# A token's norm factor enters a decoder layer's opening by a diagonal matrix on TensorE

## The chip, the cores and the metric

The kernel runs on one core of one Trainium2 chip. The metric is device time in microseconds (us) of one execution. The engines are TensorE (PE; its weight loads are listed apart, as PEld), VectorE (DVE), ScalarE (ACT), GpSimd (POOL) and SyncE (SP), which here only issues transfers. Each engine works through its own queue in order. A product on TensorE writes to PSUM, which is eight banks of 128 partitions by 512 fp32 columns.

## The reference

One layer of a decoder on 512 tokens of width 2048, all in fp32: a norm, one input projection whose columns feed gated linear attention (GLA) and differential softmax attention, an output projection, a norm and the residual, then a gated feed-forward part of 5632 with a short convolution, again between norms. The change concerns the first norm and the first 512 columns that are projected:

```
h = rmsnorm(x, attn_pre_norm)    # x * rsqrt(mean(x*x) + 1e-6) * g, by token
proj = h @ w_in                  # 512 x 2048 by 2048 x 6160
```

A token's h is x times one factor of that token, times the gain row g, which is the same for all tokens.

## The kernel before

Tokens are held in four tiles of 128 (t = 0 to 3), one token to a partition. For the projections h is needed transposed, its 2048 columns on partitions in 16 slots, and in two parts: `ah` (the value rounded to fp32r, which TensorE multiplies in one instruction) and `al` (the rest). Every weight piece of 128x1024 is split in the same way: ACT copies the high part (L148), DVE subtracts it for the low part (L149). A product is then three matmuls, ah by high, ah by low, al by high (L202 to L204, 512 columns each).

`first_half` is the opening. It computes the first 512 projected columns while x, the gain row and the first weights arrive, and it does this for the first 1024 columns of h of every tile, then for the second 1024, always in pieces of 512 columns (`H4`). Its order is written out by hand, and PE, ACT, DVE, POOL and SP run it as written:

- The gain row is brought to all partitions. Its first 1024 columns come by a small transfer to one partition and a product with a matrix that has ones in one row (`spread`, L260: an fp32 product into a bank, once for each 512 columns), and DVE copies the bank to `gb` (L261). The other 1024 come by a transfer. Transpositions of the identity (`warm`, L267) keep TensorE busy before and after.
- For each tile ACT squares x with a running sum (`square_by` for tiles 0 and 1, L275; `square` for 2 and 3, L285), DVE and POOL make of the sums the token's factor `rs` (L277, L278, L280; POOL's power is L280).
- DVE multiplies x by the factor and the gain row at once (`scale`, L292).
- PE transposes four 128x128 blocks into a bank (`turn`, through `transpose_into_act`, L169), and ACT and DVE split the bank into `ah` and `al` (L161, L162).
- PE multiplies (`prods`, `mm_n`).

So every tile goes squares, factor, scaling, transposition, split, products. For tile 0 this chain ends later than its data, and for tile 1 it begins once ACT is through with the first weights. From tile 2 on the products of the tiles before lie beside it. `transpose_into_act` is used a second time, much later, for the second norm.

Behind the opening a scheduler places the rest (the other projections, the gate and constants that are prepared meanwhile) by a model of time; from about 107 us its order on PE is the same in both programs. The later lines that the prediction names: L605 (GLA scores by block, an fp32 product of 128x128 by 128x128, once for each of four blocks and four heads), L403 (a DVE multiplication of a 128x256 tile by a number), L493 (the transposition of small constants, among them rows of the convolution's bias).

Of the kernel before, what the change touches and what calls it, by code (L numbers as in the profile page):

```python
# [9 lines left out]
F32 = mybir.dt.float32  # L10
F32R = mybir.dt.float32r
U8 = mybir.dt.uint8
AF = mybir.ActivationFunctionType
ALU = mybir.AluOpType
# [3 lines left out]
P = 128  # L18
D = 2048
S = 512  # L20
NT = S // P
# [14 lines left out]
def hybrid_layer(ctx: ExitStack, tc: tile.TileContext, x, attn_pre_norm, w_in, w_alpha_up, b_alpha,  # L36
# [3 lines left out]
    nc = tc.nc  # L40
    x2, out2 = x[0], out[0]
# [5 lines left out]
    def dma(o, i):  # L47
        return nc.sync.dma_start(out=o, in_=i)
# [3 lines left out]
    act = nc.scalar.activation  # L52
    tt = nc.vector.tensor_tensor
    ts = nc.vector.tensor_scalar
    stt = nc.vector.scalar_tensor_tensor
    mm = nc.tensor.matmul

    const = ctx.enter_context(tc.tile_pool(name="const", bufs=1))
    small = ctx.enter_context(tc.tile_pool(name="small", bufs=8, side="right"))
# [5 lines left out]
    ident = few.tile([P, P], F32, name="ident")  # L65
# [11 lines left out]
    def bank(pool=None):  # L77
        return (pool or psa).tile([P, 512], F32, name="bank", tag="bank")
# [31 lines left out]
    def load(src, a, by=None):  # L110
        raw = wpool.tile([P, GR], F32, name="raw", tag="raw", bufs=4)
        (by or nc.sync).dma_start(out=raw.rearrange("p (a b) -> p a b", a=a), in_=src)
        return raw
# [25 lines left out]
    def granule(src, a, raw=None, spare=None, hl=None):  # L139
        if raw is None:  # L140
            raw = load(src, a)
        if hl is not None:
            hi, lo = hl[:, 0, :], hl[:, 1, :]
        elif spare:
            hi, lo = spare_halves(spare)
        else:
            hi, lo = halves()
        act(hi, raw, AF.Copy)  # L148
        tt(lo, raw, hi.bitcast(F32), ALU.subtract)  # L149
        r = "p (a b) -> p a b"  # L150
        return hi.rearrange(r, a=a), lo.rearrange(r, a=a)

    def rsqrt_mean(ss, n, width=1):
        t = small.tile([P, width], F32, name="ms", tag="ms")
        nc.gpsimd.tensor_scalar(t, ss, 1.0 / n, EPS, ALU.mult, ALU.add)
        r = small.tile([P, width], F32, name="rs", tag="rs")
        nc.gpsimd.tensor_tensor(r, t, nhalf[:, :width], ALU.pow)
        return r

    def split(hi, lo, src):  # L160
        act(hi, src, AF.Copy)  # L161
        tt(lo, src, hi.bitcast(F32), ALU.subtract)  # L162

    def transpose_into_act(src, t, slot0, n):
        for g in range(0, n, 4):
            m = min(4, n - g)
            b = bank()
            for j in range(m):
                nc.tensor.transpose(b[:, j * P:(j + 1) * P], src[:, (g + j) * P:(g + j + 1) * P], ident)  # L169
            bv = b[:, :m * P].rearrange("p (k c) -> p k c", k=m)  # L170
            split(ah[:, t, slot0 + g:slot0 + g + m, :], al[:, t, slot0 + g:slot0 + g + m, :], bv)

    def bcast_row(tile_ap, row):
        dma(tile_ap, row.partition_broadcast(P))
# [23 lines left out]
    def mm_n(banks, t, g, w, slots=tuple(range(KT)), ks=(0, 1)):  # L198
        for k in ks:
            i = 2 * g + k  # L200
            st, sp, s = i == 0, i == KT - 1, slots[i]
            mm(banks[t], ah[:, t, s, :], w[0][:, k, :], start=st, stop=False)  # L202
            mm(banks[t], ah[:, t, s, :], w[1][:, k, :], start=False, stop=False)  # L203
            mm(banks[t], al[:, t, s, :], w[0][:, k, :], start=False, stop=sp)  # L204
# [15 lines left out]
    bp = boot.enter_context(tc.tile_pool(name="boot", bufs=6))  # L220

    def big8(name, dt=F32):
        return bp.tile([P, 2048], dt, name=name, tag="big8", bufs=6)


    def first_half(c):
        gb = big8("gb")
        jb = bp.tile([P, 1024], F32, name="jb", tag="jb", bufs=1)
        xts = [big8("xt") for _ in range(NT)]
        w3 = big8("w3", F32R).rearrange("p (h x) -> p h x", h=2)  # L230
        H2 = [slice(1024 * i, 1024 * (i + 1)) for i in range(2)]
        H4 = [slice(512 * i, 512 * (i + 1)) for i in range(4)]
        rs, raws, w = {}, {}, {}
        banks = [bank(psm) for _ in range(NT)]
        col = C_GV + 512 * c

        def load_x(t):
            for i in range(2):
                dma(xts[t][:, H2[i]], x2[t * P:(t + 1) * P, H2[i]])

        def load_w(*gs):
            for g in gs:
                raws[g] = load(w_in3[:, 2 * g:2 * g + 2, col:col + 512], 2)

        def weights(g):
            w[g] = granule(None, 2, raws[g], hl=w3 if g == 3 else None)

        def gain_row():
            row = gb[:, H2[1]]
            one = xts[3][:, :P]  # L250
            nc.vector.memset(row[:, :512], 0.0)
            nc.gpsimd.memset(row[:, 512:], 0.0)
            nc.vector.memset(one, 0.0)
            nc.vector.memset(one[:1], 1.0)
            nc.scalar.dma_start(out=row[:1], in_=attn_pre_norm[0:1, H2[0]])

            def spread():
                for i in range(2):
                    b = bank()
                    mm(b, one, row[:, H4[i]], start=True, stop=True)  # L260
                    nc.vector.tensor_copy(gb[:, H4[i]], b)  # L261
            return spread

        def warm(n):
            b = bank()
            for i in range(n):
                nc.tensor.transpose(b[:, (i % 4) * P:(i % 4 + 1) * P], ident, ident)  # L267

        def square_by(t, n):
            q = small.tile([P, 2], F32, name="ss2", tag="ss2", bufs=4)  # L270
            if n > 2:
                q = xts[3][:, P:P + n]
            m = 2048 // n
            for i in range(n):
                act(jb[:, :m], xts[t][:, m * i:m * (i + 1)], AF.Square, accum_out=q[:, i:i + 1])  # L275
            ss = small.tile([P, 1], F32, name="ss", tag="ss")
            nc.vector.reduce_sum(ss, q, axis=AX.X)  # L277
            ts(ss, ss, 1.0 / D, EPS, ALU.mult, ALU.add)  # L278
            rs[t] = small.tile([P, 1], F32, name="rs", tag="rs")
            nc.gpsimd.tensor_tensor(rs[t], ss, nhalf[:, :1], ALU.pow)  # L280

        def square(t):
            ss = small.tile([P, 2], F32, name="ss2", tag="ss2", bufs=4)
            for i in range(2):
                act(jb, xts[t][:, H2[i]], AF.Square, accum_out=ss[:, i:i + 1])  # L285
            sm = small.tile([P, 1], F32, name="ss", tag="ss")
            nc.gpsimd.tensor_tensor(sm, ss[:, 0:1], ss[:, 1:2], ALU.add)
            rs[t] = rsqrt_mean(sm, D)

        def scale(t, *ps):  # L290
            for i in ps:
                stt(xts[t][:, H4[i]], xts[t][:, H4[i]], rs[t], gb[:, H4[i]], ALU.mult, ALU.mult)  # L292

        def turn(t, *ps):
            for i in ps:
                transpose_into_act(xts[t][:, H4[i]], t, 4 * i, 4)

        def prods(t, *gs):
            for g in gs:
                mm_n(banks, t, g, w[g])  # L300

        spread = gain_row()
        for i in range(4):
            dma(xts[0][:, H4[i]], x2[:P, H4[i]])
        load_w(0, 1, 2, 3)
        load_x(1)
        load_x(2)
        warm(11)
        spread()
        warm(9)  # L310
        square_by(0, 4)
        load_x(3)
        bcast_row(gb[:, H2[1]], attn_pre_norm[0, H2[1]])
        scale(0, 0, 1)
        weights(0)
        turn(0, 0)
        weights(1)
        turn(0, 1)
        weights(2)
        weights(3)  # L320
        square_by(1, 2)
        prods(0, 0, 1, 2, 3)
        scale(1, 0, 1)
        turn(1, 0, 1)
        square(2)
        square(3)
        scale(2, 0, 1)
        prods(1, 0, 1, 2)
        mm_n(banks, 1, 3, w[3], ks=(0,))
        turn(2, 0, 1)  # L330
        mm_n(banks, 1, 3, w[3], ks=(1,))
        scale(3, 0, 1)
        prods(2, 0, 1)
        scale(0, 2, 3)
        turn(3, 0, 1)
        prods(2, 2)
        scale(1, 2, 3)
        turn(0, 2, 3)
        prods(2, 3)
        scale(2, 2, 3)  # L340
        turn(1, 2, 3)
        prods(3, 0, 1)
        scale(3, 2, 3)
        turn(2, 2, 3)
        prods(3, 2)
        turn(3, 2, 3)
        prods(3, 3)
        return banks
# [44 lines left out]
    for li, hs in enumerate(LEVELS):  # L393
        nb = 64 // hs
        m = ms[:, 64 * li:64 * (li + 1)]
# [25 lines left out]
    rows = tmp("rows")[:NF, :].rearrange("p (a d) -> p a d", a=4)  # L421
# [735 lines left out]
    m = [wp.tile([P, D], F32, name=f"m{t}") for t in range(NT)]  # L1157
# [808 lines left out]
```

## Time and profile before

| | |
|---|---|
| median of 3 runs | 2057.74 us (2056.23 to 2057.76) |
| the profiled execution | 2057.81 us, of which its span is 2055.7 us |
| PE busy | 2044.0 us, 99% of the span |
| DVE, ACT, POOL busy | 76%, 50%, 15% |
| data moved | 369.86 MB, 180 GB/s in the mean |

The span runs from the first instruction to the last end; the rest of the execution's time lies around it. An engine's busy time does not count its waits. The views used below are the page's first part, the busy time by stage, the waits (who waited for whom, total, times, longest), the chain of waits (which work ended last, piece after piece: start, length, engine, tile and line, "x4" for four instructions; "issue" is time in which nothing is seen to hold the engine), the timeline (start, length, and in brackets the idle time before it) and the groups of instructions by line.

### The profile page before, as it was taken

How to read it: one execution, taken by the hardware profiler on the slowest of the kernel's cores; microseconds unless marked ns; L12 is line 12 of the kernel's file. 1: busy time of each engine (PE TensorE's matmuls, PEld its weight loads, DVE VectorE, ACT ScalarE, POOL GpSimd, SP SyncE). 2: the span in 40 equal slices, each digit the busy share in tenths (PEclk: the TensorE clock that was granted, in tenths of full speed). 3: DMA queues.
4: the chain of work that ended last, by engine and by line, in shares of the span. 5: the costliest groups of instructions: out<-in, count | busy, mean ns of one | idle time of the engine just before them, and what ended most of it. 6: DMA issues, size and time to landing. Idle time of an engine off the chain costs nothing.

```text
span 2055.7 us, 36415 instructions
## 1 busy us (share of the span) xinstructions
PE 2044.0 (99%) x14757; PEld 1908.2 (93%) x14757; DVE 1561.7 (76%) x1868; ACT 1037.1 (50%) x1372; POOL 305.0 (15%) x315
## 2 busy tenths in 40 slices
PE   9999999999999999999999999999999999999999
PEld 6799999999999989899999999999999988888887
DVE  7877777766787665977777777777777888988977
ACT  5644444555555543454454454555455654544433
POOL 1022222222201110011011111111110111111100
PEclk9999999999999999999999999999999999999999
DMA  5488887888877784367577577667667796676663
GB/s 205 125 211 180 200 186 180 193 185 204 189 225 187 167 328 163 83 154 188 128 167 190 132 170 182 139 165 179 146 165 193 210 264 175 192 197 175 167 182 123
DMA packets 294830, 369.86 MB, mean 180 GB/s; under 512 B 15441, under 2 KB 239109, under 8 KB 292870
## 3 DMA queue, kind: packets, MB, share of 16 engines
q1 hardware_dynamic: 198020, 258.21, 37.3%
q0 software_dynamic: 91136, 100.68, 32.0%
q10 hardware_dynamic: 5506, 8.66, 1.2%
q8 instruction: 115, 1.88, 0.4%
q14 instruction: 53, 0.43, 0.1%
HBM read 319.78 MB, written 47.71 MB: 179 GB/s over the span
## 4 chain that ended last, share of the span: by engine, by line
PE 85%; issue 9%; DVE 2%; DMA 2%; ACT 1%; POOL 1%; POOLq 0%; ACTq 0%; DVEq 0%
PE bank L1477 10%; PE bank L1475 10%; PE bank L1476 10%; PE bank L1584 6%; PE bank L1585 6%; PE bank L1586 6%; PE bank L854 4%; PE bank L856 4%; PE bank L855 4%; PE bank L850 3%; PE bank L852 3%; PE bank L851 3%; PE bank L202 2%; PE bank L204 1%; PE bank L203 1%
## 5 line engine op out<-in xcount | busy, mean ns | idle before, releaser
L148 ACT ACTIVATE ring<-raw 128x1024 fp32r<-128x1024 f32 x317 | 336.5, 1063 | 432.7 <-PE bank L1476 117.3
L149 DVE TENSOR_TENSOR ring<-raw,ring 128x1024 fp32r<-128x1024 f32 x317 | 385.6, 1222 | 211.3 <-ACT ring L148 207.4
L148 ACT ACTIVATE ring<-rt 128x1024 fp32r<-128x1024 f32 x221 | 234.9, 1064 | 261.7 <-PE bank L1476 159.0
L1477 PE MATMUL bank<-ah,ring 128*128 128x256 f32 x1280 | 353.6, 276 | 0.8 <-DVE ring L149 0.8
L1475 PE MATMUL bank<-ah,ring 128*128 128x256 f32 x1280 | 353.4, 276 | 0.0
L1476 PE MATMUL bank<-al,ring 128*128 128x256 f32 x1280 | 353.3, 276 | 0.0
L149 DVE TENSOR_TENSOR ring<-rt,ring 128x1024 fp32r<-128x1024 f32 x221 | 269.9, 1222 | 90.4 <-ACT ring L148 89.7
L1477 PEld LDWEIGHTS bank<-ah,ring 128*128 128x128 f32 x1280 | 240.2, 188 | 1.0 <-DVE ring L149 1.0
L1475 PEld LDWEIGHTS bank<-ah,ring 128*128 128x128 f32 x1280 | 240.2, 188 | 0.3 <-ACT ring L148 0.2
L1476 PEld LDWEIGHTS bank<-al,ring 128*128 128x128 f32 x1280 | 240.3, 188 | 0.1
L1585 PE MATMUL bank<-ring,ah 128*128 128x512 f32 x424 | 165.0, 389 | 0.0
L1586 PE MATMUL bank<-ring,al 128*128 128x512 f32 x424 | 165.0, 389 | 0.0
L1584 PE MATMUL bank<-ring,ah 128*128 128x512 f32 x424 | 152.1, 389 | 0.0
L854 PE MATMUL bank<-ring,ah 128*128 128x256 f32 x448 | 129.4, 289 | 0.0
L856 PE MATMUL bank<-ring,ah 128*128 128x256 f32 x448 | 125.6, 280 | 0.0
L855 PE MATMUL bank<-ring,al 128*128 128x256 f32 x448 | 125.5, 280 | 0.0
L1423 POOL DMA_DIRECT2D raw<-in_w_ffn_in_dram x40 | 51.1, 1277 | 390.9 <-DVE ring L149 389.8
L1423 POOL DMA_DIRECT2D rt<-in_w_ffn_in_dram x40 | 50.9, 1276 | 332.3 <-DVE ring L149 269.6
L148 ACT ACTIVATE ring<-wt 128x1024 fp32r<-128x1024 f32 x60 | 63.6, 1059 | 71.2 <-PE bank L855 37.0
L1586 PEld LDWEIGHTS bank<-ring,al 128*128 128x128 f32 x424 | 79.6, 188 | 16.7
L1584 PEld LDWEIGHTS bank<-ring,ah 128*128 128x128 f32 x424 | 79.6, 188 | 16.6
L1585 PEld LDWEIGHTS bank<-ring,ah 128*128 128x128 f32 x424 | 79.6, 188 | 16.5
(427 smaller groups left out, 5843.2 us busy)
## 6 DMA issues: line engine op xcount, KB each, us to landing
raw<-in_w_ffn_in_dram SPq DMA_DIRECT2D x96, 512.0 KB, 5.2
raw<-in_w_in_dram SPq DMA_DIRECT2D x56, 512.0 KB, 3.6
raw<-in_w_ffn_out_dram SPq DMA_DIRECT2D x46, 512.0 KB, 6.0
raw<-in_w_in_dram POOLq DMA_DIRECT2D x40, 512.0 KB, 7.1
rt<-in_w_ffn_in_dram SPq DMA_DIRECT2D x40, 512.0 KB, 5.3
rt<-in_w_ffn_in_dram POOLq DMA_DIRECT2D x40, 512.0 KB, 6.2
raw<-in_w_ffn_in_dram POOLq DMA_DIRECT2D x40, 512.0 KB, 6.2
raw<-in_w_o_dram SPq DMA_DIRECT2D x24, 512.0 KB, 4.7
```

What stands on the lines that cost most here:

```text
L148: act(hi, raw, AF.Copy)
L149: tt(lo, raw, hi.bitcast(F32), ALU.subtract)
L854: mm(o, sh[:, n, kk, :], wh[:, k, :], start=st, stop=False, **NOW)
L855: mm(o, sl[:, n, kk, :], wh[:, k, :], start=False, stop=False, **NOW)
L856: mm(o, sh[:, n, kk, :], wl[:, k, :], start=False, stop=sp_, **NOW)
L1423: nc.gpsimd.dma_start(out=raws[g].rearrange("p (a b) -> p a b", a=self.a), in_=self.block(0, j, g), accum_op=ALU.add)
L1475: mm(o, wh, sh[:, :, kk, :], start=start and kk == 0 and n == 0, stop=False, **NOW)
L1476: mm(o, wh, sl[:, :, kk, :], start=False, stop=False, **NOW)
L1477: mm(o, wl, sh[:, :, kk, :], start=False, stop=kk == HK - 1, **NOW)
L1584: mm(b[j], sh[:, o:o + P], w[0][:, q, :], start=start and st == 0, stop=False, **NOW)
L1585: mm(b[j], sh[:, o:o + P], w[1][:, q, :], start=False, stop=False, **NOW)
L1586: mm(b[j], sl[:, o:o + P], w[0][:, q, :], start=False, stop=st == 3, **NOW)
```

## The change

The factor is no longer part of the scaling. DVE multiplies x by the gain row alone (`scale`, now a product of two tensors), and multiplies the identity by the tile's factor into one of four 128x128 tiles (`factor`, `diag`). The transposition of a block in the opening is now a matmul of the block with that diagonal, an ordinary fp32 product, in place of TensorE's transposition. The later use of `transpose_into_act` stays as it was.

For tile 0 the scaling reads the gain row out of the two PSUM banks in which `spread` left it, the first 512 columns ahead of the sum of squares. The copies of these banks to `gb` come later, behind the fourth weight's split. The warming transpositions use one bank throughout. Tile 1's x is loaded and squared in three pieces (1024, 512 and 512 columns) instead of two, and its partial sums have a tile of their own.

```diff
-    def transpose_into_act(src, t, slot0, n):
+    def transpose_into_act(src, t, slot0, n, by=None):
...
-                nc.tensor.transpose(b[:, j * P:(j + 1) * P], src[:, (g + j) * P:(g + j + 1) * P], ident)
+                o, i = b[:, j * P:(j + 1) * P], src[:, (g + j) * P:(g + j + 1) * P]
+                if by is None:
+                    nc.tensor.transpose(o, i, ident)
+                else:
+                    mm(o, i, by, start=j == 0, stop=j == m - 1, skip_group_check=True)
...
+        diag = bp.tile([P, NT * P], F32, name="diag", bufs=1)
+        part_sums = bp.tile([P, 8], F32, name="part_sums", bufs=1)
...
             def spread():
+                got = [bank() for _ in range(2)]
                 for i in range(2):
-                    b = bank()
-                    mm(b, one, row[:, H4[i]], start=True, stop=True)
-                    nc.vector.tensor_copy(gb[:, H4[i]], b)
+                    mm(got[i], one, row[:, H4[i]], start=True, stop=True)
+                return got
...
-        def scale(t, *ps):
+        def scale(t, *ps, by=None):
             for i in ps:
-                stt(xts[t][:, H4[i]], xts[t][:, H4[i]], rs[t], gb[:, H4[i]], ALU.mult, ALU.mult)
+                tt(xts[t][:, H4[i]], xts[t][:, H4[i]], gb[:, H4[i]] if by is None else by, ALU.mult)
+
+        def of_tile(t):
+            return diag[:, P * t:P * (t + 1)]
+
+        def factor(t):
+            ts(of_tile(t), ident, rs[t], None, ALU.mult)
...
-                transpose_into_act(xts[t][:, H4[i]], t, 4 * i, 4)
+                transpose_into_act(xts[t][:, H4[i]], t, 4 * i, 4, by=of_tile(t))
...
-        load_x(1)
+        FINER = (H2[0], H4[2], H4[3])
+        load_x(1, FINER)
...
-        spread()
+        rows = spread()
         warm(9)
-        square_by(0, 4)
+        square_by(0, H4, lambda: scale(0, 0, by=rows[0]))
...
-        scale(0, 0, 1)
+        scale(0, 1, by=rows[1])
+        factor(0)
...
         weights(3)
-        square_by(1, 2)
+        for i in range(2):
+            nc.vector.tensor_copy(gb[:, H4[i]], rows[i])
+        square_by(1, FINER)
+        scale(1, 0, 1)
+        factor(1)
         prods(0, 0, 1, 2, 3)
-        scale(1, 0, 1)
         turn(1, 0, 1)
         square(2)
         square(3)
         scale(2, 0, 1)
+        factor(2)
...
         scale(3, 0, 1)
+        factor(3)
```

What this makes of DVE's queue at tile 0, from the copies of the gain row to the first weight's split (`xt` is x of a tile, `ss` the sum of squares, `rs` the factor). Before:

```order
L261 COPY gb<-bank 128x512 x2
L277 TENSOR_REDUCE ss<-xt 128x1
L278 TENSOR_SCALAR ss<-ss 128x1
L292 SCALAR_TENSOR_TENSOR xt<-xt,rs,gb 128x512 x2
L149 TENSOR_TENSOR ring<-raw,ring 128x1024
```

And now:

```order
L299 TENSOR_TENSOR xt<-xt,bank 128x512
L284 TENSOR_REDUCE ss<-part_sums 128x1
L285 TENSOR_SCALAR ss<-ss 128x1
L299 TENSOR_TENSOR xt<-xt,bank 128x512
L305 TENSOR_SCALAR diag<-ident,rs 128x128
L149 TENSOR_TENSOR ring<-raw,ring 128x1024
```

Both copies have left this place, the sum of squares stands between the two scalings, and the diagonal is last.

DVE's queue at tile 1, from the fourth weight's split (into the tile `w_98`) to the split of tile 1's transposed banks. Before:

```order
L149 TENSOR_TENSOR w_98<-raw,w_98 128x1024
L277 TENSOR_REDUCE ss<-ss_189 128x1
L278 TENSOR_SCALAR ss<-ss 128x1
L292 SCALAR_TENSOR_TENSOR xt<-xt,rs,gb 128x512 x2
L162 TENSOR_TENSOR al<-bank,ah 128x512 x2
```

And now:

```order
L149 TENSOR_TENSOR w_98<-raw,w_98 128x1024
L337 COPY gb<-bank 128x512 x2
L284 TENSOR_REDUCE ss<-part_sums 128x1
L285 TENSOR_SCALAR ss<-ss 128x1
L299 TENSOR_TENSOR xt<-xt,gb 128x512 x2
L305 TENSOR_SCALAR diag<-ident,rs 128x128
L162 TENSOR_TENSOR al<-bank,ah 128x512 x2
```

The two copies now stand here, ahead of tile 1's sum of squares, and the diagonal follows the two scalings.

SP's queue at the end of the opening, where it goes from weights (`raw`) to small constants (`gnb`, `lt` and others), as a difference:

```order
 L112 DMA raw<-in_w_in_dram 128x2x512 x4
-L112 DMA raw<-in_w_in_dram 128x4x256 x2
+L112 DMA raw<-in_w_in_dram 128x4x256 x3
 L48 DMA gnb<-in_gla_norm_dram 128x256
 L48 DMA lt<-in_lambda_q_dram 128x128
```

One more weight load has come ahead of the constants. On PE the opening's queue keeps its order, with products by `diag` where the transpositions stood.

More of the change, by code (lines that the diff above doesn't have):

```diff
@@ L235, in first_half, with load_x @@
         col = C_GV + 512 * c
-        def load_x(t):
-            for i in range(2):
-                dma(xts[t][:, H2[i]], x2[t * P:(t + 1) * P, H2[i]])
+        diag = bp.tile([P, NT * P], F32, name="diag", bufs=1)
+        part_sums = bp.tile([P, 8], F32, name="part_sums", bufs=1)
+        def load_x(t, ps=H2):
+            for i in ps:
+                dma(xts[t][:, i], x2[t * P:(t + 1) * P, i])
         def load_w(*gs):
@@ L257, in spread, with square_by @@
             def spread():
+                got = [bank() for _ in range(2)]
                 for i in range(2):
-                    b = bank()
-                    mm(b, one, row[:, H4[i]], start=True, stop=True)
-                    nc.vector.tensor_copy(gb[:, H4[i]], b)
+                    mm(got[i], one, row[:, H4[i]], start=True, stop=True)
+                return got
             return spread
+        warm_bank = bank()
         def warm(n):
-            b = bank()
             for i in range(n):
[L267 to L275, printed above, removed]
+                nc.tensor.transpose(warm_bank[:, (i % 4) * P:(i % 4 + 1) * P], ident, ident)
+        def square_by(t, ps, between=None):
+            q = part_sums[:, 4 * t:4 * t + len(ps)]
+            for i, sl in enumerate(ps):
+                act(jb[:, :sl.stop - sl.start], xts[t][:, sl], AF.Square, accum_out=q[:, i:i + 1])
+            if between:
+                between()
             ss = small.tile([P, 1], F32, name="ss", tag="ss")
```

## The prediction

> **What bounds the kernel now.** I read the page's first part, then the engines by stage, then TensorE's waits, and last the chain of waits through the opening. The span and the first part of the page:
>
> ```profile
> span 2055.7 us, 36415 instructions
> PE 2044.0 (99%) x14757; PEld 1908.2 (93%) x14757; DVE 1561.7 (76%) x1868; ACT 1037.1 (50%) x1372; POOL 305.0 (15%) x315
> ```
>
> TensorE (PE) works 99% of the span. The view by stage, for PE alone (stretch, its length, PE's busy time and count, granted clock, share of the DMA engines, GB/s), says where the other 1% lies:
>
> ```profile
> 0.00:11.42 11.42, 7.54 (x24) 1.00 0.79 270
> 11.42:21.43 10.01, 9.05 (x41) 1.00 1.03 418
> 21.43:46.00 24.57, 24.57 (x132) 1.00 0.33 111
> 46.00:731.00 685.00, 684.71 (x5169) 1.00 0.79 188
> ```
>
> From 21.43 us on PE has no idle time in the opening, and next to none for 700 us after it: whatever the change adds to PE behind 21.43 us lengthens the kernel one for one, and whatever it saves on VectorE (DVE) or ScalarE (ACT) there is worth nothing. Time can be won only ahead of 21.43 us. PE's waits for the line that the change touches, the transpositions (total, times, longest):
>
> ```profile
> PE bank L169 <- DVE xt L292: 2.0, 2, 1.4
> ```
>
> These two, 1.4 and 0.6 us, are the waits of token tile 0 and of token tile 1 for their scaled rows. The chain of waits shows what they hang on (start, length, what):
>
> ```profile
> 8.91 0.69 DVE gb L261
> ...
> 9.94 0.56 POOL rs L280
> 10.53 0.76 DVE xt L292
> 11.29 0.14 issue
> 11.42 0.64 PE bank L169 x4
> ...
> 12.09 0.60 ACT ah L161
> 12.68 0.95 ACT ring L148
> ...
> 15.90 1.15 ACT jb L275 x2
> ...
> 17.08 1.17 ACT jb L275 x2
> ...
> 18.69 0.56 POOL rs L280
> 19.28 0.76 DVE xt L292
> ...
> 20.08 0.67 PE bank L169 x4
> 20.84 0.63 PE bank L169 x4
> 21.46 0.46 PE bank L202
> ```
>
> Tile 0: the second copy of the gain row (8.91), then the norm's factor (9.94 to 10.50), then the scaling (10.53), then PE (11.42). Tile 1: from ACT's first split (12.09) ACT runs through to the squares of tile 1 (15.90 to 18.25), then factor, scaling, PE (20.08).
>
> **Term 1, on PE: 64 transpositions become 64 products.** A transposition is one PE instruction. An fp32 product by a diagonal is two, as the profile counts the kernel's other fp32 products. The two groups (count, busy time, mean of one, idle before), and below them the chain at one place of each:
>
> ```profile
> L169 PE MATMUL bank<-ident,xt 128*128 128x128 f32 x64 | 8.8, 275 | 2.1 <-DVE xt L292 2.0
> L605 PE MATMUL bank<-gq,gk 128*128 128x128 f32 x32 | 4.2, 274 | 0.0
> ```
> ```profile
> 30.48 0.23 PE bank L202
> ...
> 31.16 0.88 PE bank L169 x8
> ```
> ```profile
> 176.34 0.89 PE bank L605 x8
> ```
>
> L605 is issued 16 times (four heads, four blocks of 128x128), and has 32 rows: two each. Its operands are of the same shape and type as those of the new product. The means (275 and 274 ns) are latencies and say nothing of pace; the chain does: eight transpositions take 0.88 us of PE, and four products (eight rows) 0.89. So a turn of eight blocks goes from 0.88 to 2 x 0.89 = 1.78 us, 0.90 more. There are eight turns (four tiles, two halves). Six lie behind 21.43 us, where PE is full: 6 x 0.90 = 5.4 us; 5.0, if a group of eight pays once, not twice, for some 0.07 us at its ends, is my low end. The other two lie on the path of term 2.
>
> The row first, then the page: four products took 0.89 us. The Trainium skill, FP8 and Floating Point Precision, section TensorE Precision Notes, states that a true fp32 product is four passes through the array. At 0.23 us for a one-pass row of 512 columns (L202) a pass of 128 columns would be 0.058, four products 0.92, a turn 1.84, and this term 6 x 0.96 = 5.8 us by the page, as an estimate, beside 5.4 by the row.
>
> **Term 2, the path ahead of 21.43 us.** What the moved steps rest on:
>
> ```profile
> 7.21 0.69 DVE L261 COPY gb<-bank 128x512 f32<-128x512 f32 x1 [5.29 <-PE bank L260]
> ```
> ```profile
> 7.14 0.19 ACT L275 ACTIVATION_READ_ACCUMULATOR jb<-xt 128x1 f32 x1
> ```
> ```profile
> 8.67 1.15 PEld L267 LDWEIGHTS bank<-ident 128*128 128x128 f32 x8 [0.62 <-issue]
> ```
> ```profile
> L162 DVE TENSOR_TENSOR al<-bank,ah 128x512 fp32r<-128x512 f32 x16 | 10.4, 682 | 2.1 <-ACT ah L161 2.1
> L253 DVE MEMSET xt<- 128x128 f32 x1 | 0.2, 165 | 0.0
> ```
> ```profile
> 48.47 0.37 DVE L403 TENSOR_SCALAR gnb<-gnb 128x256 f32<-128x256 f32 x1
> ```
>
> *Tile 0.* At 7.21, where a copy out of PSUM stood, DVE now multiplies the first 512 columns by the bank itself; L162, a DVE product with one operand in PSUM, takes 0.68, the copy took 0.69, so it ends at 7.90. The sum of squares no longer stands behind the second copy: ACT's last partial sum is there at 7.33. From the second copy's end (9.60) to the factor (10.50) took 0.90, so the factor is there at 8.80. The second 512 columns wait for the second broadcast as the copy did, 8.91 to 9.60. Then the diagonal: no row shows it; a fill of the same 128x128 took 0.165 and an operation of the same kind on 128x256 took 0.37. I take 0.24, between them. Ready at 9.84; with the 0.14 us of issue that the chain shows, PE starts at about 9.95 instead of 11.42 (its warming transpositions, loaded until 8.67 + 1.15 = 9.82, are just over). Lead: 1.5 us.
>
> *Tile 0's turn and ACT.* The first bank holds four products, 0.45 us more than four transpositions. So ACT's first split starts at about 11.05 instead of 12.09: the lead is 1.0. The inputs are there: 270 GB/s to 11.42 us are 3.08 MB, x of tile 0 and the four first weight loads are 3.15, and tile 1's 1.05 MB follow at 418 GB/s by about 14.2, ahead of its squares at 14.9.
>
> *Tile 1.* Its squares now come in three pieces, not two. A piece of 512 took 0.83 (tile 0's), a piece of 1024 1.18: 2.84 instead of 2.35, from 14.9 to 17.7. DVE meanwhile has more to do ahead of the reduction:
>
> ```profile
> 16.54 1.22 DVE L149 TENSOR_TENSOR w<-raw,w 128x1024 fp32r<-128x1024 f32 x1
> ```
> ```profile
> 4.87 0.63 ACT L275 ACTIVATE jb<-xt 128x512 f32<-128x512 f32 x1 [0.16 <-DMA xt<-in_x_dram]
> 5.41 0.19 ACT L275 ACTIVATION_READ_ACCUMULATOR jb<-xt 128x1 f32 x1
> 5.70 0.63 ACT L275 ACTIVATE jb<-xt 128x512 f32<-128x512 f32 x1
> ```
>
> The fourth weight's low half ended at 17.76, now at 16.7; behind it stand the two copies of the gain row (2 x 0.69), to 18.1; the reduction and its neighbour, 0.35; two scalings (2 x 0.68) to 19.8; then the diagonal, to 20.0. The factor, 0.98 behind the reduction as before (18.27 to 19.25), is ready at 19.1 and waits. PE starts tile 1 at 19.9 to 20.1, against 20.08: the two copies and the two scalings, which DVE has to run ahead of the diagonal, eat the lead. Tile 1's first bank is 0.45 slower as well, which puts its split and the first product (21.46) 0.3 us late; before, though, the second half waited for its own scaling (20.84), and now does not, so PE's own end comes at 20.0 + 1.78 = 21.8. Both say 0.3 late with my rounded gaps, and 0.1 early where each gap is 0.1 shorter. I take 0.1 late, and -0.6 to +0.5 as ends: all of the idle time of tile 1 gone at one end, the diagonal at 0.37 at the other.
>
> **What costs nothing.** The lighter scaling (a product of two for one of three operands) and two more diagonals on DVE: DVE is not what PE waits for behind 21.43 us. The persistent warming bank and the two gain banks: the copies free these by 18.1, before PE needs them for tile 1 at 20. x of tile 1 in three transfers: the same bytes. The scheduled part behind the opening is reordered up to about 107 us, none of it late for a full PE, with one exception, rival 2.
>
> **The sum.** 5.4 + 0.1 = 5.5 us. The profiled execution took 2057.81 us (span 2055.7 and 2.1 around it), 0.07 above the median of the three runs, 2057.74: 2057.81 + 5.5 = 2063.3.
>
> **Rivals.** *1. Passes of 128 columns go at the pace of the one-pass products.* At 0.23 us for 512 columns (L202, above), two passes of 128 would take 0.115, as much as a transposition (0.11): term 1 would vanish and the first two turns would not grow, which leaves the lead of 0.3 to 0.6 us: 2057.4, not slower. It decides once a turn costs under 1.56 us (4.1 / 6 = 0.68 above 0.88). Against it stand the rows of L605; for it, only that no row has a diagonal for an operand. 5%.
>
> *2. The third weight load on SP.* SP's queue now issues three, not two, loads of 128x4x256 ahead of the small constants, and the third waits for DVE to free a buffer. The constants are needed by PE at a fixed place:
>
> ```profile
> 44.27 0.34 SPq L48 DMA_DIRECT2D gnb<-in_gla_norm_dram  x1
> ...
> 50.07 0.35 SPq L48 DMA_DIRECT2D rows<-in_conv_b_dram  x1
> ```
> ```profile
> 54.60 0.22 PE L493 MATMUL bank<-ident,ba 4*128 4x4 f32 x1
> ```
>
> PE comes there 5.5 us later (60.1). The last row of constants is issued 5.8 after the first, and lands some 2 to 3 us on, so a first issue later than about 51.5 makes PE stand. I expect 49 to 50 (44.27 and the delay of the turns). Beyond that each us costs a us: 2065 with two. 7%.
>
> *3. The lead is kept.* If DVE runs copies and scalings in its gaps between the splits, tile 1 starts at its factor's time, 18.4, and its first product 1.3 us early: 5.4 - 1.3 = 4.1, 2061.9, on the bound of no change. Against it: DVE takes its instructions in the order that the program gives, and these four stand behind the fourth weight. 10%.
>
> **Chances.** Forecast 78%, rivals 5, 7 and 10. About 0.2% (4.1 us) is what a measurement of this kernel can tell from no change, so slower by more begins at 2061.9. The forecast's own ends, 5.0 - 0.6 and 5.4 + 0.5, are 2062.2 and 2063.7; of its 78 I give 9 to less than 4.1, since its low end is near and a median of few runs moves (the three runs lie 1.5 us apart). Rival 2 lies beyond, rival 3 half and half, rival 1 within but for one in a hundred. Slower 0.69 + 0.07 + 0.05 = 0.81, the same 0.09 + 0.05 + 0.04 = 0.18, faster 0.01. The range, 2061.2 to 2065.0, takes in the forecast's ends, most of rivals 2 and 3, and leaves out rival 1.
>
> **What would show it.** Right: 128 PE rows for 64 products, about 1.78 us of PE for each turn of eight; PE's first turn at about 9.9 and its second at about 20.0, with PE idle for over 1 us ahead of the second; PE without idle time from 22 us on, and every later stage shifted by the same 5 to 6 us. Wrong: a turn of under 1.6 us; tile 1's turn before 19.3; PE waiting at the constants' transposition near 60 us.

## The result and the profile after

The change makes the kernel slower: a median of 2063.31 us over 13 runs (2061.45 to 2074.99) against 2057.19 us over 13 runs of the kernel before (2055.49 to 2059.45), ratio 1.0032 with a 95% interval of 1.0024 to 1.0041 (the two medians alone give 1.0030). The highest run had a granted clock of 0.949 where the others had 0.999 to 1.0. The profiled execution took 2062.0 us, 4.2 more than that of before. The page's first part, after:

```profile
span 2060.2 us, 36544 instructions
PE 2049.0 (99%) x14821; PEld 1915.6 (93%) x14821; DVE 1564.2 (76%) x1872; ACT 1033.2 (50%) x1372; POOL 304.9 (15%) x315
```

PE has 64 rows more, one for each product that was a transposition, and 5.0 us more of busy time. The other engines hardly moved. The groups of instructions by line, up to 60 us, show the 64 products as 128 rows, with the same latency as the 64 transpositions had (276 ns, before 275):

```profile
L173 PE MATMUL bank<-diag,xt 128*128 128x128 f32 x128 | 15.7, 276 | 1.5 <-issue 1.2 <-DVE diag L305 0.3
```

What a turn of eight blocks costs is in the chain of waits. Before, five of the six turns behind tile 1 took 0.87 or 0.88, and the first took 0.96. That first one and another:

```profile
26.76 0.96 PE bank L169 x8
33.42 0.87 PE bank L169 x8
```

The same six turns, after:

```profile
26.43 1.78 PE bank L173 x16
31.63 1.78 PE bank L173 x16
34.79 1.78 PE bank L173 x16
37.95 1.78 PE bank L173 x16
42.47 1.78 PE bank L173 x16
45.63 1.78 PE bank L173 x16
```

The chain through the opening, after:

```profile
2.18 5.10 DMA xt<-in_x_dram
...
7.36 0.73 ACT jb L280 x2
...
8.12 0.17 DVE ss L284
...
8.55 0.56 POOL rs L287
9.11 0.03 issue
9.13 0.30 DVE diag L305
9.43 0.04 issue
9.47 1.17 PE bank L173 x8
```

PE's first turn starts at 9.47 instead of 11.42. But what it hangs on is new: the chain no longer begins with the gain row, it begins with the landing of x of tile 0. Tile 1 on DVE and then PE, from the timeline (start, length, in brackets the idle time before it):

```profile
16.26 1.28 DVE L337 COPY gb<-bank 128x512 f32<-128x512 f32 x2
17.46 0.14 DVE L284 TENSOR_REDUCE ss<-part_sums 128x1 f32<-128x3 f32 x1
...
17.70 1.28 DVE L299 TENSOR_TENSOR xt<-xt,gb 128x512 f32<-128x512 f32 x2
18.91 0.28 DVE L305 TENSOR_SCALAR diag<-ident,rs 128x128 f32<-128x128 f32 x1
```
```profile
19.29 2.02 PE L173 MATMUL bank<-diag,xt 128*128 128x128 f32 x16 [1.23 <-issue]
...
21.10 0.50 PE L206 MATMUL bank<-ring,ah 128*128 128x512 f32 x1
```

The diagonal is the last thing on DVE, behind copies and scalings, and PE stood 1.23 us. The row names "issue" and no engine, but PE starts 0.10 us behind the diagonal's end (19.19), so I take the diagonal for what it waited for; an experiment below moves the two together. PE's first product of tile 1 starts at 21.10; before, in the same view, at 21.43. So of 1.95 us of lead at the first turn 0.33 are left here.

I use two marks from here on: that product, and the start of PE's first product of the next projection, at 107.06 before and at 112.07 after. The busy time by stage between them, first before, then after (length, PE busy and count, clock, DMA):

```profile
21.43:107.06 85.63, 85.63 (x402) 1.00 0.41 128
```
```profile
21.10:112.07 90.97, 90.97 (x452) 1.00 0.41 126
```

PE is full from end to end in both, and the stretch has grown by 5.34 us: six times 0.89. PE's other groups of rows have the same counts in both stretches; only the turns have more (49 rows of L169 before, 98 of L173 after, with those of tile 1's turn that still run at the first border). Less the 0.33 of lead that gives the 5.0 us at the second mark.

### The profile page after: what moved, and what is told of

The parts are those of the page before. It is cut to its first block, busy times and chain, and to the rows that moved or that the text cites. A ratio compares the mean times of both kernels' runs of the same rounds, so it can differ in the third digit from the quotient of the medians.

```text
span 2060.2 us, 36544 instructions
## 1 busy us (share of the span) xinstructions
PE 2049.0 (99%) x14821; PEld 1915.6 (93%) x14821; DVE 1564.2 (76%) x1872; ACT 1033.2 (50%) x1372; POOL 304.9 (15%) x315
## 4 chain that ended last, share of the span: by engine, by line
PE 93%; DVE 3%; DMA 2%; ACT 1%; issue 1%; POOL 0%; SPq 0%; POOLq 0%; DVEq 0%; ACTq 0%
PE bank L1495 12%; PE bank L1497 12%; PE bank L1496 12%; PE bank L1605 6%; PE bank L1606 6%; PE bank L1604 6%; PE bank L874 4%; PE bank L875 4%; PE bank L876 4%; PE bank L870 3%; PE bank L872 3%; PE bank L871 3%; PE bank L190 2%; PE bank L188 2%; PE bank L189 2%; PE bank L207 2%
## 5 line engine op out<-in xcount | busy, mean ns | idle before, releaser
L876 PE MATMUL bank<-ring,ah 128*128 128x256 f32 x448 | 125.7, 281 | 0.0
```

The source lines that it names most:

```text
L876: mm(o, sh[:, n, kk, :], wl[:, k, :], start=False, stop=sp_, **NOW)
```

## Experiments

Theory A is the prediction's: the two rows of each fp32 product, on a PE that is full, are the growth. Theory B puts it on DVE's longer queue ahead of tile 1 and on the reordered schedule behind the opening, with the products covered.

**One product a turn.** The change's opening with seven of eight blocks transposed, so that the norm's factor is left out for them:

```diff
-                if by is None:
+                if by is None or j or slot0 % 8:
                     nc.tensor.transpose(o, i, ident)
                 else:
-                    mm(o, i, by, start=j == 0, stop=j == m - 1, skip_group_check=True)
+                    mm(o, i, by, start=True, stop=True, skip_group_check=True)
```

> The changed kernel with its whole opening as it is, but of the eight blocks of a turn only the first is multiplied by the diagonal; the other seven are transposed with the identity, so the norm's factor is left out for them. Mark: the start of PE's first product of the next projection, 107.06 us before and 112.07 after the change. Theory A (the two rows of each fp32 product on a full PE are the whole growth): a turn is 9 rows, 0.99 us, not 1.78; six turns give back 4.7, tile 1 comes 0.3 earlier and its turn is 0.8 shorter, so the mark is at 106.3, ahead of the kernel before. Theory B (DVE's longer queue ahead of tile 1 and the reordered schedule behind the opening are the growth, products are covered): the mark stays at 111 to 112.

The stretch between the marks:

```profile
20.22:106.61 86.39, 86.39 (x407) 1.00 0.47 138
```

86.39 is 0.76 more than before (six more rows at 0.11 would be 0.66), and 4.6 less than after. The second mark is at 106.61, 0.3 behind the 106.3 expected and still ahead of the kernel before, with DVE's queue, the late copies and the diagonals all in place. The part of theory B that lies on DVE is out. The other part, the reordered schedule, is not tested here: the scheduler placed the work behind the opening otherwise, and SP issues the first small constant at 43.82, near the 44.27 of before and not at 48.82 as after the change. One run, 2055.49 us, as fast as the fastest run of before.

**The products alone, in the kernel before.**

```diff
-                nc.tensor.transpose(b[:, j * P:(j + 1) * P], src[:, (g + j) * P:(g + j + 1) * P], ident)
+                o, i = b[:, j * P:(j + 1) * P], src[:, (g + j) * P:(g + j + 1) * P]
+                if by is None:
+                    nc.tensor.transpose(o, i, ident)
+                else:
+                    mm(o, i, by, start=j == 0, stop=j == m - 1, skip_group_check=True)
...
-                transpose_into_act(xts[t][:, H4[i]], t, 4 * i, 4)
+                transpose_into_act(xts[t][:, H4[i]], t, 4 * i, 4, by=ident)
```

> The kernel before with one edit: the 64 transpositions of the opening become fp32 products by the identity; scaling, factor and DVE's order stay. Theory A: six turns 0.90 longer each, 5.4 us, and 0.9 more on the path of tiles 0 and 1: the mark goes from 107.06 to 113.4. Theory B: the mark stays within 0.5 of 107.06.

```profile
21.53:112.56 91.03, 91.03 (x452) 1.00 0.42 124
```

The stretch is 91.03, as after the change, without any of its other parts. The 0.9 on the path that I expected on top did not come: tile 1's first product is at 21.53, only 0.1 late. In this execution PE's first turn started at 10.52, 0.9 earlier than in the trace of before, since DVE could copy the gain row's second bank at 8.01 instead of 8.91, with the same code ahead of it; from that turn to tile 1's product it took 11.0 us against 10.0, and that is the 0.9 to 1.0. One run, 2062.73 us.

**Products in the six late turns only.** As above, with one line different:

```diff
+                transpose_into_act(xts[t][:, H4[i]], t, 4 * i, 4, by=None if t < 2 and i < 2 else ident)
```

> The kernel before with products by the identity in the six turns that lie behind 21.43 us, and transpositions in the first two (tile 0 and tile 1, first half). Theory A: the opening to 21.46 us is untouched, the mark moves by 6 x 0.90 = 5.4 to 112.5, and the time by the same, ratio 1.0026. Theory B: mark and time as before.

```profile
21.73:112.71 90.98, 90.98 (x451) 1.00 0.41 122
```

90.98, 5.35 more than before, with the same code ahead of it. The time is 2061.66 us (10 runs) against 2057.28 for the kernel before on the same chip, ratio 1.0022 (1.0013 to 1.0031); the 1.0026 expected lies inside. With no more than the products in six turns the kernel is slower.

The products do bring the change's order along: SP issues the first small constant at 49.46 here and at 49.31 in the experiment before. So no run holds the order apart from the products. That the order adds nothing rests on PE's rows: between the marks PE has no idle time in either kernel, its other groups have the same counts, and each turn is 0.8 to 0.9 longer.

**The diagonal for tile 0 alone.** Seven turns are transposed, with factor and gain in one scaling, and tiles 1 to 3 get no diagonal:

```diff
-                transpose_into_act(xts[t][:, H4[i]], t, 4 * i, 4, by=of_tile(t))
+                transpose_into_act(xts[t][:, H4[i]], t, 4 * i, 4, by=of_tile(0) if t == 0 and i < 2 else None)
...
-                tt(xts[t][:, H4[i]], xts[t][:, H4[i]], gb[:, H4[i]] if by is None else by, ALU.mult)
+                if by is not None:
+                    tt(xts[t][:, H4[i]], xts[t][:, H4[i]], by, ALU.mult)
+                else:
+                    stt(xts[t][:, H4[i]], xts[t][:, H4[i]], rs[t], gb[:, H4[i]], ALU.mult, ALU.mult)
```

> The changed kernel with the diagonal for tile 0's first half alone; the seven other turns are transpositions again, and their scaling takes factor and gain at once, as before the change. Theory A: PE's first turn starts at 9.5 as after the change, tile 1's at about 19.3 (factor at 18.4, one scaling of 0.75), first product of tile 1 at 20.7 against 21.46, and nothing is lost behind it: mark at 106.3, time 0.8 us under the kernel before, ratio 0.9996. Theory B: as DVE's queue ahead of tile 1 still holds the two copies, most of the growth stays, mark at 109 or later.

```profile
21.30:106.95 85.65, 85.65 (x402) 1.00 0.43 130
```

Behind tile 1 nothing is lost, as expected: 85.65, and the mark is at 106.95, where theory B had 109 or later. The lead is smaller than expected: PE's first turn came at 10.15, not 9.5, and tile 1's product at 21.30, not 20.7. The time is 2057.16 us against 2057.28, ratio 0.9997 (0.9988 to 1.0006): no difference that can be measured. Why the first turn comes at another time in every trace is in ACT's timeline. The square of x of tile 0's last quarter, in the kernel before, after the change, in this kernel, and in the next experiment:

```profile
6.60 0.63 ACT L275 ACTIVATE jb<-xt 128x512 f32<-128x512 f32 x1 [0.18 <-DMA xt<-in_x_dram]
```
```profile
7.36 0.63 ACT L280 ACTIVATE jb<-xt 128x512 f32<-128x512 f32 x1 [0.71 <-DMA xt<-in_x_dram]
```
```profile
8.04 0.63 ACT L280 ACTIVATE jb<-xt 128x512 f32<-128x512 f32 x1 [1.22 <-DMA xt<-in_x_dram]
```
```profile
8.81 0.63 ACT L280 ACTIVATE jb<-xt 128x512 f32<-128x512 f32 x1 [2.38 <-DMA xt<-in_x_dram]
```

The transfer lands between 6.6 and 8.8 us, at another time in each of the nine traces; what moves it is not shown. In the trace of before the factor had to wait for the second copy of the gain row, to 9.60, and all of these landings would have been hidden under it. The end of that copy moves as well: with the same code it is at 8.70 and 9.91 in the two experiments that start from the kernel before, and PE's first turn at 10.52 and 11.73. Now the sums themselves are waited for (with one product a turn, the second broadcast), and PE's first turn comes anywhere from 9.08 (one product a turn) to 10.92 (the next experiment). Against the 11.42 of the one trace of before that is a lead of 2.3 to 0.5 us.

**The copies behind tile 1.** The change with the gain row in the accumulators' banks of tiles 2 and 3, and its copies moved:

```diff
-                got = [bank() for _ in range(2)]
+                got = banks[2:]
...
-        for i in range(2):
-            nc.vector.tensor_copy(gb[:, H4[i]], rows[i])
         square_by(1, FINER)
-        scale(1, 0, 1)
+        scale(1, 0, by=rows[0])
+        scale(1, 1, by=rows[1])
         factor(1)
+        for i in range(2):
+            nc.vector.tensor_copy(gb[:, H4[i]], rows[i])
```

> The changed kernel with the gain row's two banks taken from the accumulators of tiles 2 and 3 (not used before 26 us), tile 1's first half scaled straight from these banks too, and the two copies moved behind tile 1's diagonal. The distance from PE's first turn to tile 1's turn was 9.82 us after the change. If the two copies hold up the diagonal by all that DVE spends on them: 9.82 - 1.28 = 8.5. If the squares on ACT, which ended 0.3 before the copies, are next: 9.4 to 9.5. From the first product of tile 1 to the mark stays at 90.9 either way, since the products stay.

Tile 1 on DVE, from the timeline:

```profile
18.63 0.16 DVE L284 TENSOR_REDUCE ss<-part_sums 128x1 f32<-128x3 f32 x1 [0.84 <-ACT jb L280]
18.82 0.15 DVE L285 TENSOR_SCALAR ss<-ss 128x1 f32<-128x1 f32 x1
18.89 1.27 DVE L299 TENSOR_TENSOR xt<-xt,bank 128x512 f32<-128x512 f32 x2
20.08 0.28 DVE L305 TENSOR_SCALAR diag<-ident,rs 128x128 f32<-128x128 f32 x1
20.28 1.28 DVE L341 COPY gb<-bank 128x512 f32<-128x512 f32 x2
```

From PE's first turn (10.92) to tile 1's (20.42) took 9.50 us instead of 9.82: the copies, 1.28 us long, cost 0.3, since without them DVE waits 0.84 for ACT's squares. Between the marks 90.98. One run, 2064.18 us.

**A version meant to beat both.** The late copies, the diagonal for tile 0 alone, tile 1 scaled by factor and gain at once out of the banks, its squares in two pieces. To the edit of the diagonal for tile 0 alone this adds:

```diff
-                got = [bank() for _ in range(2)]
+                got = banks[2:]
...
-                if by is not None:
+                if t == 0 and by is not None:
                     tt(xts[t][:, H4[i]], xts[t][:, H4[i]], by, ALU.mult)
                 else:
-                    stt(xts[t][:, H4[i]], xts[t][:, H4[i]], rs[t], gb[:, H4[i]], ALU.mult, ALU.mult)
+                    stt(xts[t][:, H4[i]], xts[t][:, H4[i]], rs[t], gb[:, H4[i]] if by is None else by,
+                        ALU.mult, ALU.mult)
...
-        FINER = (H2[0], H4[2], H4[3])
-        load_x(1, FINER)
+        load_x(1)
...
-        for i in range(2):
-            nc.vector.tensor_copy(gb[:, H4[i]], rows[i])
-        square_by(1, FINER)
+        square_by(1, H2)
         prods(0, 0, 1, 2, 3)
-        scale(1, 0, 1)
+        scale(1, 0, by=rows[0])
+        scale(1, 1, by=rows[1])
+        for i in range(2):
+            nc.vector.tensor_copy(gb[:, H4[i]], rows[i])
```

> The same banks and late copies, but the diagonal for tile 0's first half alone; everything else is transposed as before the change, tile 1's first half scaled by factor and gain at once out of the banks, its squares in two pieces. From PE's first turn to tile 1's turn 9.2 us, first product of tile 1 at about 20.1 against 21.43 before, 85.6 from there to the mark, as before: mark at 105.8. Time 1.3 us under the kernel before, ratio 0.9994, which the timing can hardly tell from 1.

PE's timeline at tile 1:

```profile
19.64 1.38 PE L171 MATMUL bank<-ident,xt 128*128 128x128 f32 x8 [0.60 <-DVE xt L302]
20.99 0.50 PE L206 MATMUL bank<-ring,ah 128*128 128x512 f32 x1
21.32 0.40 PE L207 MATMUL bank<-ring,ah 128*128 128x512 f32 x1
22.10 0.50 PE L208 MATMUL bank<-ring,al 128*128 128x512 f32 x1 [0.38 <-DVE al L162]
```

From the first turn (10.46) to tile 1's took 9.18, as expected, but x landed late in this execution (8.36 for the last quarter), and the copies now stand ahead of the split of tile 1, which costs 0.38. The second mark is at 107.00, not 105.8. Time 2057.07 us against 2057.6, ratio 0.9999 (0.999 to 1.0008): no faster than the kernel before, as far as the timing can tell.

**The change once more.**

> The changed kernel once more, for a second trace. If the growth of 5.0 us at the mark is the change's own, it is there again within 0.5 (the first transfers' landing moves the whole opening), and from tile 1's first product to the mark 90.9 to 91.0. The waits that PE has behind the mark (0.5 at 400 us, 0.8 at 592, 0.3 at 735 in the first trace) should differ if they are chance, and stay at their places if the new order makes them.

```profile
21.41:112.39 90.98, 90.98 (x452) 1.00 0.43 125
```

2062.76 us (10 runs) against 2057.6, ratio 1.0028 (1.0019 to 1.0037). The stretch is 90.98 again. PE's first turn was at 9.79, tile 1's at 19.60 (9.81 apart, 9.82 in the first trace), and the second mark 5.33 late, as x came 0.3 later. PE's waits behind the mark, here:

```profile
PE bank L963 <- DVE p L951: 0.8, 1, 0.8
PE bank L876 <- DVE ring L149: 0.8, 1, 0.8
```

Of the two traces of the change, the wait of L876 is in this one alone, and those at 400 and 735 us are gone: by the mark set beforehand these are chance. The wait of L963 (near 592 us) is in both. It is in all five traces with products in the six late turns (0.80 to 0.88 us), and at most 0.28 in the other four, so it is no chance of one execution but comes with the products and their order. The whole does not show it: from the second mark to PE's last row it took 1941.7 and 1941.9 us with the change and 1942.7 before; over all nine traces 1940.4 to 1943.8, with products or without.

## Why the prediction was right

**Term 1** (six turns, 0.90 each, on a full PE: 5.4 us) is the growth: 5.34, and 5.35 to 5.40 in every other kernel with all six. The row that priced it, four fp32 products in 0.89 us, gave 1.78 for a turn, and each of the six is 1.78. The low end of 5.0 assumed that eight rows pay some 0.07 us at their ends; no row shows this, and 16 rows took twice the time of eight. The Trainium skill's four passes (FP8 and Floating Point Precision, section TensorE Precision Notes), at the pace of the one-pass row, gave an estimate of 1.84 a turn and 5.8 in all: near the measured 1.78 and 5.34, but the row was nearer.

**Term 2** (the path ahead of tile 1: 0.1 late, ends -0.6 to +0.5) came out 0.33 early in the first trace and 0.02 early in the second, against the one trace of before. That is no more than an unchanged opening moves: with six late turns as products, tile 1's first product came at 21.73, against 21.43.

The step that failed is tile 0's. "ACT's last partial sum is there at 7.33" was one execution's landing taken for a fixed time, under a cover (the copy that ended at 9.60) which the change took away. It was 8.09 in the trace of the change and up to 9.5 in the experiments. The second broadcast at 8.91, which the prediction had PE hang on (diagonal at 9.84, PE at 9.95), was one execution's time as well: after the change the second scaling ran at 8.39, right behind the sums, so the broadcast was no longer last, and PE's turn came at 9.47. In the second trace it came at 9.79, close to the foretold 9.95, but by the path through the sums; that nearness is luck.

That the lead is eaten ahead of tile 1 was right (9.82 us between the turns, 10.05 foretold); the copies' share in it is 0.3 us, by the kernel that moved them, and the rest of the diagonal's delay lies with ACT's squares and the two scalings. The diagonal took 0.28, for 0.24 assumed, but DVE's whole stretch from the copies to its end took 2.9 us (16.26 to 19.19) where 3.3 was foretold.

**The rivals.** Passes at the one-pass pace: no, 1.78. The third weight load: SP issued the first constant at 48.82 us, 0.2 ahead of the foretold 49 to 50, and PE came to the constants without waiting:

```profile
59.60 0.22 PE L513 MATMUL bank<-ident,ba 4*128 4x4 f32 x1
```

The lead kept: no, 0.33 and 0.02.

**The sum.** 2063.3 was foretold, and the median is 2063.31. That is closer than the parts deserve: medians of before moved from 2057.19 to 2057.6 between sets of runs, the growth from 6.1 to 5.2, and the traces show 5.0 and 5.3 at the second mark and only 4.0 and 4.5 at PE's last row. What makes the first set's 6.1 more than the traces account for was not settled; the waits behind the mark change from trace to trace and sum to 1.8 us in both traces of the change and to 1.9 in that of before.

## What to carry to other kernels

On an engine that is full, price an instruction by the pace at which its like follow each other, not by the length of a row: the transposition and the fp32 pass both show 275 ns, both follow each other every 0.11 us, and the product by a diagonal is two of them. A trick that shortens a latency belongs only at the place where the engine waits: here PE waited for scaled rows in two turns of eight, and all eight paid. Even at that place alone the trick gained nothing that could be measured (ratio 0.9997). When a wait is taken off the path, look at what it covered, and whether that has a fixed time at all; the landing of x had none here.

## What the runs showed of the hardware

The power of the factor on POOL, an operation on 128x1, took 0.55 us in most places of the opening, and 0.93 where DVE multiplied two SBUF tensors beside it. POOL's timeline, in the change and in the kernel whose scalings read PSUM for the second operand:

```profile
17.87 0.93 POOL L287 TENSOR_TENSOR rs<-ss,nhalf 128x1 f32<-128x1 f32 x1 [8.77 <-DVE ss L285]
```
```profile
19.05 0.55 POOL L287 TENSOR_TENSOR rs<-ss,nhalf 128x1 f32<-128x1 f32 x1 [8.51 <-DVE ss L285]
```

0.93 stood in all three traces in which such scalings ran beside it, 0.55 in the one whose scalings read PSUM and 0.55 or 0.56 in the five in which DVE waited for the factor. The same power later in the trace of the change (L157) took 1.43 to 1.55 beside DVE products of 128x1024 in SBUF (at 207, 358, 408 and 781 us), and 0.55 beside operations with an operand in PSUM (at 197 and 362). But it also took 1.06 at 367 us with DVE idle, so this is not the only thing that slows it. In the opening it cost nothing, since the diagonal came behind the scalings anyway. I had not expected it, no experiment was made on it alone, and the cause is not shown.
